# 96 bytes of padding in place of 32 ahead of the constants in a two-layer diffusion backbone

## Chip, cores and metric

One Trainium2 chip, one of its cores. The metric is the device time of one execution in microseconds (us); the median of three runs of the kernel before is 2884.68 us.

## What is computed

The reference is a backbone of two layers over 1024 latent tokens (T) and 256 context tokens (CT), 1280 together (TA), with D = 1024 channels, in float32:

```python
for i in range(DEPTH):                       # 2 layers
    h  = modulate(rmsnorm(x, norm_mix_w[i]), sh_m, sc_m)
    hc = modulate(rmsnorm(ctx, norm_mix_w[i]), shc_m, scc_m)
    y, y_c = ab_mixer(...) if i % 2 == 0 else cd_mixer(...)
    x = x + g_m * y
    ...
    x = x + g_f * swiglu(modulate(rmsnorm(x, norm_ffn_w[i]), sh_f, sc_f), w_gate, w_up, w_down)
    ...                                      # layer 0 does the same for ctx
return rmsnorm(x, final_norm_w)
```

Layer 0 mixes with a gated token MLP and neighbourhood attention (`ab_mixer`), layer 1 with a Fourier transform and gated linear attention (`cd_mixer`). The FFN's hidden width is 2816, 22 slabs of 128.

## The kernel before, in words

**Three matmuls for one.** Every float32 operand of a large product is held as two tiles of type float32r, a high and a low part. `mm3` (lines 45 to 51) issues three matmuls into one PSUM target: `wh` on `xh` (L49), `wh` on `xl` (L50), `wl` on `xh` (L51). In `nc.tensor.matmul(out, wh, xh)` the second argument is the stationary operand, which is loaded into the array ahead of the matmul (LDWEIGHTS), and the third is the moving operand, which streams through it. For most products the weights are stationary, 128 columns of them, and the activations move, 512 columns (a block of 512 tokens) or 256 (the context block). The value products `gv`, `gu`, `av` and `va` have it the other way: slices of the activations are stationary, 256 or 272 columns of weights move.

**Stages** of the program, by the time at which they run: layer 0's norms, projections and gated MLP to about 300 us; attention (`natten`) to 690 us, with the other projections (`qk`) and half of the output product (`ho`) put between its steps by a generator (`s.bg`, `tick`); `out_proj` to 760 us; the first FFN to 1640 us; layer 1's linear attention, `gla_*`, and the Fourier part `fnet` to 2110 us, again with a generator beside them; `out_proj`; the second FFN from 2190 us to the end, with the final norm behind its last blocks. In an FFN (`ffn`, line 330 on) `up` makes the gate and up products (`pg` is the PSUM name of both in the trace) and `down` the product `dn`, whose result is added to `xT` by DVE (`residual`, L316).

**What sets the order.** Each engine executes its instructions in the order of the program; a tile framework adds the waits. The order is that of the Python code with its generators, and none of it depends on addresses.

**Where tiles lie.** Pools are stacks. Those on the left side grow up from the lowest free byte of a partition, those on the right side grow down from byte 229,344. `cp` is the first pool on the left; its first tile is `pad`, 8 floats (32 bytes) that nothing reads (`setup`, line 113), then `ident`, `ones` and the small constants. Behind `cp` on the left come `hm` (the activations `hh`/`hl`, eight pairs of 4 KB; in layer 1 the same places hold `xT`, the Fourier twiddles `tw` and the mixed activations `mixd`) and `hc` (the eight pairs of context activations, 1 KB each, behind a 192-byte tile `cs`). On the right are the weights (`whi`, `wlo`), eight slots of 5 KB (`xT` in layer 0, `mixc` in layer 1, and others) and the FFN's hidden tiles (`hhi`, `hlo`).

The *residue* of an operand is the byte at which it begins in its partition, modulo 128. From the built program:

| operand | first byte before | residue before | residue after |
|---|---|---|---|
| `hh`, `hl`, `mixd` (and `xT`, `tw` in layer 1), left | from 19,872 | 32 | 96 |
| `hc`, left | from 85,600 | 96 | 32 |
| `whi`, `wlo`, right | from 162,272 | 96 | 96 |
| `mixc`, right | from 188,384 | 96 | 96 |
| `hhi`, `hlo` of the FFNs, right | from 85,728 | 96 | 96 |
| `vhi`, `vlo` of the gated MLP (moving in `gt`), right | 120,224 | 32 | 32 |
| `swh`, `swl` (stationary in `gt`), right | 113,792 | 0 | 0 |

The matmuls with float32r operands, by columns and by the residues of the moving and the stationary operand:

| columns | moving, stationary before | after | count | which |
|---|---|---|---|---|
| 512 | 32, 96 | 96, 96 | 4704 | `pg` on `hh`/`hl` 2112, `pg` on `mixd` 1056, `qk` 384, `ho` 384, `op` 192, `gqk` 192, `gf` 192, gates 192 |
| 512 | 96, 96 | the same | 3320 | `dn` 2112, `pg` on `mixc` 1056, `op` 144, `dec` 8 |
| 512 | 32, 0 | the same | 24 | `gt` |
| 256 | 96, 96 | 32, 96 | 1488 | context blocks on `hc`, 1056 of them `pg` |
| 256 | 96, 32 | 96, 96 | 1152 | `gv`, `gu`, `av` and a few `qk`, stationary `hh`/`hl` |
| 256 | 96, 96 | 96, 32 | 288 | the same, stationary `hc` |
| 256 | 32, 96 | 96, 96 | 192 | `y` on `tw` |
| 256 | 96, 96 | the same | 1676 | attention's `sp` and `o`, `dn` of the context, others |

Of the kernel before, what the change touches and what calls it, by code (L numbers as in the profile page):

```python
# [11 lines left out]
F32 = mybir.dt.float32  # L12
# [8 lines left out]
P = 128  # L21
# [48 lines left out]
def psum(s, tag, name=None):  # L70

    if tag != "s":
        return s.ps.tile([P, 512], F32, name=name or tag, tag=tag, bufs=2 if tag == "t" else 1)
    if s.half is None:
        pair = psum2(s, name)
        s.half = pair[:, 512:]
        return pair[:, :512]
    half, s.half = s.half, None
    return half
# [30 lines left out]

def setup(s, a):
    nc, cp = s.nc, s.cp
    cp.tile([P, 8], F32, name="pad")
    s.ident = cp.tile([P, P], F32, name="ident")
    make_identity(nc, s.ident)
    s.ones = cp.tile([P, P], F32, name="ones")
    nc.gpsimd.memset(s.ones, 1.0)
    s.half_neg = cp.tile([P, 16], F32, name="half_neg")
    nc.gpsimd.memset(s.half_neg, -0.5)


    flat = lambda ap, n: bass.AP(tensor=ap.tensor, offset=ap.offset, ap=[[P, n], [1, P]])
    r0 = s.xp.tile([16, P], F32, name="r0")
    nc.sync.dma_start(r0[0:8, :], flat(a["c"], 8))
    nc.sync.dma_start(r0[8:16, :], flat(a["c_ctx"], 8))
    s.cs = s.hc.tile([P, KT, 6], F32, name="cs")
    nc.gpsimd.memset(s.cs, 0.0)
    pt = psum(s, "t", "setup")
    nc.tensor.transpose(pt[:, :16], r0, s.ident[:16, :16])
    nc.scalar.activation(s.cs[:, :, 2:4], pt[:, :16].rearrange("p (s k) -> p k s", s=2), AF.Silu)  # L130

    r1 = s.xp.tile([P, P], F32, name="r1")
    nc.gpsimd.memset(r1, 0.0)
    rows = [("nmw", a["norm_mix_w"], 16), ("nfw", a["norm_ffn_w"], 16), ("dbf", a["cd_decay_b_fwd"], 2),
            ("dbb", a["cd_decay_b_bwd"], 2), ("hnw", a["cd_head_norm_w"], 1), ("sgb", a["ab_sgu_b"], 4)]
    at = 0
    for name, ap, n in rows:
        nc.sync.dma_start(r1[at:at + n, :], flat(ap, n))
        at += n
    r2 = s.xp.tile([96, P], F32, name="r2")  # L140
    nc.sync.dma_start(r2, flat(a["ada_b"], 96))
    pt = psum(s, "t", "setup")
    nc.tensor.transpose(pt[:, :P], r1, s.ident)
    nc.tensor.transpose(pt[:, P:P + 96], r2, s.ident[:96, :96])
    s.cols = cp.tile([P, 41], F32, name="cols")
    nc.vector.tensor_copy(s.cols, pt[:, :41])
    s.adab = cp.tile([P, 96], F32, name="adab")
    nc.vector.tensor_copy(s.adab, pt[:, P:P + 96])
    at = 0
    s.col = {}  # L150
    for name, ap, n in rows:
        s.col[name] = s.cols[:, at:at + n]
        at += n
    s.mod = [cp.tile([P, 48, 2], F32, name=f"mod{l}") for l in range(2)]
    s.acol = [[cp.tile([P, KT, 2], F32, name=f"acol{l}{j}") for j in range(2)] for l in range(2)]
# [1217 lines left out]
def body(ctx, tc, a, out, dbg=None):  # L1373
# [22 lines left out]
    with P_("hc", side="left") as s.hc:  # L1396
# [6 lines left out]
        with ExitStack() as es:  # L1403
# [4 lines left out]
            with R("ld") as ld, R("np0") as s.np_:  # L1408
                s.xp = s.adap = ld
                setup(s, a)  # L1410
                jobs = [q(0), k(0)]
                s.bg = ada(s, a, 0, [1, 0], "pe")
                xin, r = [], {}
                for i in range(TA // P):
                    xin.append(load_x(s, a, i))
                    tick(s)
                    if i == 7:
                        acol(s, 0, 0)
                    if i in (3, 7, 9):
                        blk = BLK[(i - 2) // 3]  # L1420
                        turn_x(s, xin, xT, blk)
                        r[blk] = rstd(s, xT, blk)
                tick(s, 3)
                ws = proj_w(s, a, jobs)
                drain(s)
                hT = [tuple(Cols(m, s.hc.tile([P, CT], F32R, name=f"hc{x}{k}")) for x, m in enumerate(pair))
                      for k, pair in enumerate(alloc_h(s))]
                proj_t(s, a, hT, jobs, pre=lambda blk: norm(s, xT, hT, 0, 0, blk, r[blk]), ws=ws)
                spill(s, xT, xd[0])
# [180 lines left out]
```

## Time and profile before

| | |
|---|---|
| median of 3 runs | 2884.68 us (2879.55 to 2887.2) |
| the profiled execution's own time | 2882.54 us |
| its span, first to last instruction | 2880.6 us |
| granted TensorE clock, mean | 0.991 of full speed |
| PE (matmul) busy | 2779.9 us, 97%, 14927 matmuls |
| DVE / ACT / POOL busy | 54% / 31% / 7% |
| chain that ended last | PE 80%, DVE 8%, ACT 4%, DMA 4%, issue 2% |

How to read it: the span is the profiled execution's time without what lies around it. Matmuls are pipelined and the ends of their records are modelled, so records overlap and a busy PE is not PE at its peak; the distance between the starts of neighbouring matmuls is what a matmul takes of the engine's time. PEld is the loading of stationary operands, which runs beside the matmuls. The chain is followed back from the last instruction, at each step to what released it. The trace names tiles without buffer numbers: `pg<-hh,whi` is a matmul with the stationary operand `whi` and the moving operand `hh` into PSUM tile `pg`.

### The profile page before, as it was taken

How to read it: one execution, taken by the hardware profiler on the slowest of the kernel's cores; microseconds unless marked ns; L12 is line 12 of the kernel's file. 1: busy time of each engine (PE TensorE's matmuls, PEld its weight loads, DVE VectorE, ACT ScalarE, POOL GpSimd, SP SyncE). 2: the span in 40 equal slices, each digit the busy share in tenths (PEclk: the TensorE clock that was granted, in tenths of full speed). 3: DMA queues.
4: the chain of work that ended last, by engine and by line, in shares of the span. 5: the costliest groups of instructions: out<-in, count | busy, mean ns of one | idle time of the engine just before them, and what ended most of it. 6: DMA issues, size and time to landing. Idle time of an engine off the chain costs nothing.

```text
span 2880.6 us, 38369 instructions
## 1 busy us (share of the span) xinstructions
PE 2779.9 (97%) x14927; PEld 2336.3 (81%) x14927; DVE 1550.4 (54%) x2791; ACT 893.1 (31%) x1899; POOL 198.2 (7%) x233
## 2 busy tenths in 40 slices
PE   8999999899999999999999999998999999999998
PEld 3888888787888888888888787787878888888887
DVE  4655777676664643645633466756773333333435
ACT  3442566554311111111111145554251111111112
POOL 0000222221100000000000021212010000000000
PEclk9999999999999999999999999999999999999999
DMA  8545656674231321312211143533621111111111
GB/s 300 169 130 160 180 158 178 205 211 126 81 95 52 96 80 45 103 44 88 88 37 40 35 166 87 161 121 100 222 83 52 44 46 54 48 44 51 52 44 66
DMA packets 285686, 298.50 MB, mean 104 GB/s; under 512 B 33416, under 2 KB 228673, under 8 KB 285505
## 3 DMA queue, kind: packets, MB, share of 16 engines
q1 hardware_dynamic: 285505, 296.06, 34.0%
q8 instruction: 118, 1.93, 0.3%
q14 instruction: 63, 0.52, 0.1%
HBM read 228.09 MB, written 64.49 MB: 102 GB/s over the span
## 4 chain that ended last, share of the span: by engine, by line
PE 80%; DVE 8%; ACT 4%; DMA 4%; issue 2%; POOL 1%; SPq 0%; DVEq 0%; POOLq 0%; ACTq 0%
PE pg L51 13%; PE pg L50 13%; PE pg L49 13%; PE dn L49 6%; PE dn L50 5%; PE dn L51 5%; PE o L750 2%; PE pt L720 1%; DMA adaw<-in_ada_w_dram 1%; PE sp L661 1%; PE qk L49 1%; PE ho L49 1%; PE qk L50 1%; DVE xT L316 1%; DVE wlo L57 1%
## 5 line engine op out<-in xcount | busy, mean ns | idle before, releaser
L56 ACT CAST whi<-wraw 128x1024 fp32r<-128x1024 f32 (+2 forms) x186 | 188.4, 1013 | 687.1 <-PE dn L50 404.2
L316 DVE SCALAR_TENSOR_TENSOR xT<-dn,mod,xT 128x512 f32<-128x512 f32 (+1 forms) x448 | 300.0, 686 | 122.9 <-PE dn L51 121.8
L57 DVE TENSOR_TENSOR wlo<-wraw,whi 128x1024 fp32r<-128x1024 f32 (+2 forms) x186 | 220.3, 1187 | 248.1 <-ACT whi L56 246.6
L49 PE MATMUL dn<-hhi,whi 128*128 128x512 f32 (+1 forms) x896 | 328.3, 367 | 4.6 <-DVE xT L316 3.1
L50 PE MATMUL dn<-hlo,whi 128*128 128x512 f32 (+1 forms) x896 | 327.0, 365 | 0.0
L51 PE MATMUL dn<-hhi,wlo 128*128 128x512 f32 (+1 forms) x896 | 326.7, 365 | 0.0
L346 DVE TENSOR_TENSOR sg<-sg,pg 128x512 f32<-128x512 f32 (+1 forms) x110 | 69.4, 631 | 378.7 <-ACT sg L345 378.6
L51 PE MATMUL pg<-hh,wlo 128*128 128x512 f32 x688 | 272.8, 397 | 0.2
L49 PE MATMUL pg<-hh,whi 128*128 128x512 f32 x688 | 272.5, 396 | 0.0
L50 PE MATMUL pg<-hl,whi 128*128 128x512 f32 x688 | 271.9, 395 | 0.0
L183 DVE SCALAR_TENSOR_TENSOR adaacc<-adaw,cs,adaacc 128x1024 f32<-128x1024 f32 x140 | 175.0, 1280 | 114.5 <-DMA adaw<-in_ada_w_dram 111.1
L345 ACT ACTIVATE sg<-pg 128x512 f32<-128x512 f32 (+1 forms) x110 | 60.8, 552 | 563.1 <-PE pg L51 563.1
L49 PEld LDWEIGHTS dn<-hhi,whi 128*128 128x128 f32 x896 | 168.9, 188 | 36.1 <-DVE xT L316 7.2
L51 PEld LDWEIGHTS dn<-hhi,wlo 128*128 128x128 f32 x896 | 168.9, 188 | 27.3
L50 PEld LDWEIGHTS dn<-hlo,whi 128*128 128x128 f32 x896 | 169.0, 189 | 26.8
L51 PEld LDWEIGHTS pg<-hh,wlo 128*128 128x128 f32 x688 | 129.2, 188 | 32.2 <-DVE wlo L57 1.1
L50 PEld LDWEIGHTS pg<-hl,whi 128*128 128x128 f32 x688 | 129.1, 188 | 30.3
L49 PEld LDWEIGHTS pg<-hh,whi 128*128 128x128 f32 x688 | 129.1, 188 | 30.1
L50 PE MATMUL pg<-mixd,whi 128*128 128x512 f32 x344 | 136.0, 395 | 0.0
L49 PE MATMUL pg<-mixd,whi 128*128 128x512 f32 x344 | 135.5, 394 | 0.0
L51 PE MATMUL pg<-mixd,wlo 128*128 128x512 f32 x344 | 135.5, 394 | 0.0
L49 PE MATMUL pg<-mixc,whi 128*128 128x512 f32 x344 | 134.2, 390 | 0.9 <-DVE xT L316 0.9
(569 smaller groups left out, 6192.0 us busy)
## 6 DMA issues: line engine op xcount, KB each, us to landing
adaw<-in_ada_w_dram SPq DMA_DIRECT2D x96, 512.0 KB, 3.9
wraw<-in_ffn_w_gate_dram SPq DMA_DIRECT2D x44, 512.0 KB, 3.8
wraw<-in_ffn_w_up_dram SPq DMA_DIRECT2D x44, 512.0 KB, 3.8
wraw<-in_ffn_w_down_dram SPq DMA_DIRECT2D x44, 512.0 KB, 3.8
wraw<-in_ab_w_in_dram SPq DMA_DIRECT2D x20, 512.0 KB, 5.5
xd<-xT SPq DMA_DIRECT2D x16, 640.0 KB, 5.8
xs<-xd SPq DMA_DIRECT2D x32, 256.0 KB, 3.3
xd<-xs SPq DMA_DIRECT2D x32, 256.0 KB, 2.8
```

Of the source, the lines that this page charges most:

```text
L49: nc.tensor.matmul(out, wh, xh, start=start, stop=False)
L50: nc.tensor.matmul(out, wh, xl, start=False, stop=False)
L51: nc.tensor.matmul(out, wl, xh, start=False, stop=stop)
L56: s.nc.scalar.copy(hi, src)
L57: (s.nc.gpsimd if eng == "pool" else s.nc.vector).tensor_tensor(lo, src, f32(hi), ALU.subtract)
L183: nc.vector.scalar_tensor_tensor(acc[:, v], w, c, acc[:, v], ALU.mult, ALU.add)
L316: s.nc.vector.scalar_tensor_tensor(xT[k][:, o:o + n], ps, s.mod[l][:, 8 * vec + k, sel:sel + 1], xT[k][:, o:o + n], ALU.mult, ALU.add)
L345: nc.scalar.activation(sg[:, :n], pg[:, :n], AF.Silu)
L346: nc.vector.tensor_tensor(sg[:, :n], sg[:, :n], pu[:, :n], ALU.mult)
L661: nc.tensor.matmul(sp[:, o:o + n], qq[:, x, :], kk[:, t0:t0 + n], start=x == 0, stop=x == 1)
L720: nc.tensor.transpose(pt[:n, jj * P:(jj + 1) * P], y[:, c:c + n], s.ident)
L750: nc.tensor.matmul(o_ps[:, ba * P:bz * P], vv[:n, kt, :], at(x, sl)[:n, 0, ba:bz, :].rearrange("p b q -> p (b q)"), start=q == 0 and x == ...
```

## The change

The unread tile ahead of the constants has 24 floats in place of 8, 96 bytes in place of 32:

```diff
 def setup(s, a):
     nc, cp = s.nc, s.cp
-    cp.tile([P, 8], F32, name="pad")
+    cp.tile([P, 24], F32, name="pad")
     s.ident = cp.tile([P, P], F32, name="ident")
```

Every other tile of the left side begins 64 bytes later; no tile of the right side moves. The instructions and their order are the same on every engine.

## Rows read from the trace of the kernel before

**Rows 1.** The page's head and its section 1, busy us, share and instructions.

```profile
span 2880.6 us, 38369 instructions
PE 2779.9 (97%) x14927; PEld 2336.3 (81%) x14927; DVE 1550.4 (54%) x2791; ACT 893.1 (31%) x1899; POOL 198.2 (7%) x233
```

**Rows 2.** Stretches: us, busy PE, PEld, DVE, ACT, POOL, clock, DMA share, GB/s.

```profile
760.00:1640.00 880.00, 877.16 (x4587) 745.29 (x4586) 432.93 (x566) 144.95 (x203) 0.00 (x0) 1.00 0.23 70
2190.00:2860.00 670.00, 669.96 (x2956) 548.71 (x2955) 252.99 (x323) 113.04 (x152) 1.11 (x2) 1.00 0.15 46
300.00:690.00 390.00, 368.49 (x2387) 323.38 (x2386) 278.83 (x850) 224.15 (x663) 81.80 (x105) 0.99 0.64 186
...
1740.00:2110.00 370.00, 347.16 (x1915) 292.28 (x1914) 252.20 (x519) 181.99 (x433) 55.26 (x63) 0.97 0.47 143
```

**Rows 3.** The chain of waits by line, in 2190 to 2860 us and 300 to 690 us.

```profile
by line: PE pg L50 21.6%; PE pg L49 21.5%; PE pg L51 21.5%; PE dn L50 11.6%; PE dn L49 11.6%; PE dn L51 11.6%; PE ft L1309 0.5%; ACT fsq L1311 0.1%; DVE xT L316 0.1%; DVE fss L1312 0.0%; issue 0.0%; ACTq L1311 0.0%
by line: PE o L750 12.7%; PE pt L720 9.4%; PE sp L661 7.5%; PE qk L49 5.5%; PE qk L50 4.9%; PE qk L51 4.8%; issue 4.0%; DMA wraw<-in_ab_w_out_dram 3.7%; PE ho L49 3.3%; PE ho L50 3.1%; PE ho L51 3.1%; DVE pa L731 2.3%; PE op L50 2.2%; PE op
```

**Rows 4.** Timeline of PE, second FFN: start us, us, engine, line, out<-in (`mixc`, then `mixd`).

```profile
2289.77 0.39 PE L49 MATMUL pg<-mixc,whi 128*128 128x512 f32 x1
...
2295.21 0.39 PE L49 MATMUL pg<-mixd,whi 128*128 128x512 f32 x1
...
2298.48 0.39 PE L51 MATMUL pg<-mixd,wlo 128*128 128x512 f32 x1
```

**Rows 5.** PE's groups by line and shape: count, busy us, mean ns, idle before.

```profile
L51 PE MATMUL pg<-hh,wlo 128*128 128x512 f32 x688 | 272.8, 397 | 0.2
L49 PE MATMUL pg<-hh,whi 128*128 128x512 f32 x688 | 272.5, 396 | 0.0
L49 PE MATMUL dn<-hhi,whi 128*128 128x512 f32 x688 | 268.3, 391 | 3.6 <-DVE xT L316 2.2 <-DVE sg L346 1.4
...
L51 PE MATMUL dn<-hhi,wlo 128*128 128x512 f32 x688 | 267.7, 389 | 0.0
L50 PE MATMUL pg<-mixd,whi 128*128 128x512 f32 x344 | 136.0, 395 | 0.0
...
L50 PE MATMUL pg<-mixc,whi 128*128 128x512 f32 x344 | 134.5, 391 | 0.0
```

**Rows 6.** Timeline of PE: five `gt` matmuls, the first and the next behind them.

```profile
182.67 0.39 PE L49 MATMUL gt<-vhi,swh 128*128 128x512 f32 x1
...
183.83 0.30 PE L49 MATMUL av<-whi,hh 128*128 128x256 f32 x1
```

**Rows 7.** Timeline of PE, first FFN: `pg` on `hh`/`hl`, then `pg` on `hc`.

```profile
1058.83 0.39 PE L50 MATMUL pg<-hl,whi 128*128 128x512 f32 x1
...
1061.39 0.28 PE L49 MATMUL pg<-hc,whi 128*128 128x256 f32 x1
...
1062.93 0.28 PE L50 MATMUL pg<-hc,whi 128*128 128x256 f32 x1
```

**Rows 8.** Timeline of PE, 256 columns: `gv` with stationary `hh`, `y` with moving `tw`.

```profile
115.48 0.28 PE L49 MATMUL gv<-whi,hh 128*128 128x256 f32 x1
...
117.84 0.28 PE L51 MATMUL gv<-whi,hl 128*128 128x256 f32 x1
...
2045.58 0.28 PE L51 MATMUL y<-tw,zl 128*128 128x256 f32 x1
...
2046.75 0.40 PE L49 MATMUL ho<-mixd,whi 128*128 128x512 f32 x1
```

**Rows 9.** DVE's L316 in the two FFN stretches: min/median/max ns, forms, idle before.

```profile
L316 DVE SCALAR_TENSOR_TENSOR xT<-dn,mod,xT x241: 473/743/752, 814.3 to 1638.2; 128x512 f32<-128x512 f32 x81, 128x256 f32<-128x256 f32 x40
...
  PE dn L51: 48.1, 102
...
L316 DVE SCALAR_TENSOR_TENSOR xT<-dn,mod,xT x174: 475/751/753, 2204.7 to 2859.5; 128x512 f32<-128x512 f32 x168, 128x256 f32<-128x256 f32 x6
...
  PE dn L51: 67.7, 117
```

## What I predict

> **What bounds the kernel now.** I read the head of the page first, for the share of each engine, then a table of stretches, then the chain of waits inside two stretches, and last the timeline of TensorE, because the change moves bytes and no instruction and can only show in how far apart equal instructions start.
>
> The page says that TensorE is busy 97% of a span of 2880.6 us [rows 1]. [...] In the attention stretch (300 to 690 us) it is 368.5 of 390, in the linear-attention and Fourier stretch (1740 to 2110 us) 347.2 of 370, with some 22 us without a matmul in each. The chain agrees: in the second FFN nearly all of it is matmuls `pg` and `dn` (three times 21.5% and three times 11.6%), while in the attention stretch the longest entries are small matmuls and issue and DMA each hold some 4% [rows 3]. So in the FFNs the time is the number of matmuls times the distance between their starts; elsewhere a part of what PE saves will be waited away.
>
> PE's busy figures are no help for the price: each record is longer (0.39 us) than the distance to the next start, since matmuls overlap. The distance is what counts. In one chain of the second FFN, 24 matmuls on `mixc` start from 2289.77 to 2295.21 us, 5.44 us or 0.2267 us each; then, with the weights in the same tiles and PSUM targets of the same kind, 14 matmuls on `mixd` take until 2298.48 us, 3.27 us or 0.2336 us each [rows 4]. Their rows are alike in engine, line and shape; what differs is where the moving operand lies: `mixc` begins at residue 96 of 128, as the weights do, `mixd` at residue 32 (the table of residues above). The first FFN shows the same: 11 matmuls on `hh` and `hl` (residue 32) from 1058.83 to 1061.39 us are 0.2327 us apart [rows 7]. Over all records the mean durations repeat it [rows 5]: `pg` on `hh` 396 and 397 ns and on `mixd` 395 ns, but `dn` 389 and 391 ns and `pg` on `mixc` 391 ns, whose operands both begin at 96.
>
> **Is it the residue, or the place?** `mixc` and the FFN's hidden tiles lie high in SBUF, `hh` and `mixd` low, so a difference by region would look the same. One small group speaks to that: the `gt` matmuls of the gating read a moving tile at residue 32 that lies at 120,224 bytes, above `dn`'s tiles of the second FFN, with weights at residue 0. Five starts from 182.67 to 183.83 us are 0.232 us apart [rows 6], the slow distance. That favours the residue, but on five instructions, with a distance of 32 bytes and not of 64, so I leave a chance for the region.
>
> **The change part by part.**
>
> *512-column matmuls, FFN.* Of the 4704 that go from 32 against 96 to 96 against 96, 3168 are `pg`: 2112 on `hh` and `hl`, 1056 on `mixd`. The gain of one lies between 4 ns (the smallest difference of mean durations, 395 against 391 [rows 5]) and 7 ns (0.2336 against 0.2267 us [rows 4]); in the first FFN it is 0.2327 against 0.2267, 6 ns [rows 4, 7]. I take 6 ns, the middle of the three and the one from the stage with the most of them. 3168 x 6 ns = 19.0 us, all on the path, since nothing else ends the chain there. Bounds 12.7 us (4 ns) and 22.2 us (7 ns).
>
> *512-column matmuls elsewhere.* 4704 - 3168 = 1536: projections `qk`, `gqk`, `gf`, gates, and the output products `ho` and `op`. At 6 ns they free 9.2 us of PE. The attention and later stretches have PE without a matmul for 22 of 390 and 23 of 370 us [rows 2], so most of the time there the next matmul is ready; but the small matmuls between them wait for softmax and for DMAs, and a projection that ends sooner then only lengthens such a wait. I count 60%, 5.5 us; bounds 0 and 1536 x 7 ns = 10.8 us.
>
> *256-column matmuls.* The context tiles `hc` go the other way, from 96 to 32: 1488 matmuls of 256 columns. And 1152 matmuls of 256 columns get their stationary operand (slices of `hh` and `hl`) at 96 in place of 32. The trace has all three pairs at 256 columns: 96 on 96 (`pg` on `hc`) 13 starts in 1.54 us, 0.1185 us [rows 7]; moving 96 on stationary 32 (`gv`) 20 starts in 2.36 us, 0.1180 us; moving 32 on stationary 96 (`y`) 10 starts in 1.17 us, 0.1170 us [rows 8]. They lie within 1.5 ns, and with the other sign: the unequal pairs are not slower here. The first edit is then worth 1488 x -1.5 = -2.2 us, the second 1152 x +0.5 = +0.6 us. Differences this small are about the 0.01 us to which starts are shown, so I take 0 for both together. Bounds: -3 us, and +10 us if the 7 ns of a 512-column matmul were paid by each of the 1488.
>
> *Other engines.* Tiles of the left side that DVE, ScalarE and GpSimd touch move by 64 bytes too. DVE's residual update writes `xT` at residue 96 in the first FFN and at 32 in the second; its 512-column form is the slowest in both, 752 and 753 ns [rows 9], so I cost these moves at nothing. Were they dearer, DVE's idle time in the FFNs would cover it: before that line alone it waits 48.1 and 67.7 us for PE [rows 9]. No DMA, wait or instruction is added, moved or removed, no tile changes its size, and the 64 bytes come out of free space.
>
> *Sum.* 19.0 + 5.5 + 0 = 24.5 us. The profiled execution took 2882.54 us, 1.9 us more than its span; 2882.5 - 24.5 = 2858.0 us. That execution lies 2.1 us under the median of the runs shown (2884.68), so the forecast for the median is **2860 us**, 0.85% less.
>
> **The rivals.**
>
> *Waited away outside the FFNs.* All that is gained outside is lost to later waits, and `hc` costs some ns. For it: the chain of the attention stretch with its DMA and issue pieces [rows 3]. Against: PE has a matmul running 94% of that stretch [rows 2]. 3168 matmuls at 5 to 6 ns less 1488 at up to 4 ns is 10 to 19 us: 2866 to 2875 us.
>
> *Nothing happens.* If the 6 ns belong to the region of SBUF, or to something that `mixd` and `hh` share other than the residue, the tiles stay where they are but for 64 bytes and the time is 2884.7 us, with -3 to +3 us from the 256-column forms. For it: all but the `gt` rows allow it. Against: the `gt` rows [rows 6], and that within a chain the distance changes at the very matmul at which the tile does [rows 4]. [...]
>
> *Equal residues are the costly case.* At 256 columns the equal pair has the longest distance, 0.1185 against 0.1170 us [rows 7, 8]. If that is the effect of the residue at any width, and the 6 ns of the 512-column forms are one of region (as in the rival above), then the 4704 matmuls that the change makes equal lose, for twice the columns, 2 x 1.5 = 3 ns each: 4704 x 3 ns = +14.1 us, less 2.2 us for `hc`: 2884.7 + 11.9 = 2897 us. It decides if a 512-column `pg` on `mixd` comes out over 0.2336 us. Against it: `mixc` and `dn` are equal pairs now and are the fast ones [rows 4, 5], and `gt`.
>
> **How the numbers follow.** A difference under 0.3%, 8.7 us, is about what a measurement of this kernel can't tell from none, so faster means under 2876 us and slower over 2893 us. Chances: the forecast 0.72, waited away 0.14, nothing 0.10, costly 0.04. The first two are faster: **0.86**; nothing is the same: **0.10**; the last is slower: **0.04**. The range: its low end takes all bounds to the good, 22.2 + 10.8 + 3 = 36 us, 2849 us, less 2 us for the spread of single runs: 2847. Its high end takes in the second case: 2874 us. That leaves out the last two cases and a small part of the others, not more than 2 in 10.
>
> **What would show it.** Right: `pg` on `hh` and `mixd` with mean durations of 389 to 391 ns like `mixc` and `dn`; starts 0.2267 us apart through the change from `mixc` to `mixd`; the two FFN stretches shorter by some 12 and 6 us (2112 and 1056 matmuls at 6 ns), with the number of instructions and PE's order as before; `hc` within 2 ns of 0.1185 us. The 60% is wrong if PE's idle time outside the FFNs stays as it is (all 9 us are kept) or grows by 9 us (none is). The prediction fails if `pg` on `mixd` keeps its 395 ns, or if `hc`'s distance rises towards 0.125 us.

## The result, and the profile after

Six executions of each kernel, side by side: **2862.51 us** after (2850.39 to 2863.98) against 2881.53 us before (2875.99 to 2887.2). The ratio is 0.9926, with a 95% interval of 0.9906 to 0.9946: 0.74% faster, 16 to 27 us. The forecast was 2860 us in a range of 2847 to 2874.

The head, section 1 and the shares of the chain on the page of the kernel after, to be held against [rows 1]:

```profile
span 2862.0 us, 38369 instructions
PE 2758.1 (96%) x14927; PEld 2339.4 (82%) x14927; DVE 1551.5 (54%) x2791; ACT 892.2 (31%) x1899; POOL 196.5 (7%) x233
...
PE 79%; DVE 9%; DMA 5%; ACT 4%; issue 3%; POOL 1%; SPq 0%; DVEq 0%; ACTq 0%; POOLq 0%
```

The number of instructions is the same, weight loading (PEld) is as busy as before, and PE's matmuls alone are shorter, by 21.8 us of busy time. PE's groups by line and shape in the kernel after (count, busy us, mean ns, idle before), as in [rows 5]:

```profile
L51 PE MATMUL pg<-hh,wlo 128*128 128x512 f32 x688 | 269.2, 391 | 0.6 <-DVE wlo L57 0.6
L49 PE MATMUL pg<-hh,whi 128*128 128x512 f32 x688 | 269.0, 391 | 0.0
...
L51 PE MATMUL dn<-hhi,wlo 128*128 128x512 f32 x688 | 267.6, 389 | 0.0
L50 PE MATMUL pg<-mixd,whi 128*128 128x512 f32 x344 | 134.3, 390 | 0.0
...
L50 PE MATMUL pg<-mixc,whi 128*128 128x512 f32 x344 | 133.8, 389 | 0.0
```

`pg` on `hh` went from 396 and 397 ns to 391, on `mixd` from 395 to 390; `dn`, which the change does not touch, stayed. The same passage from `mixc` to `mixd` in the timeline of the second FFN, after, as in [rows 4]:

```profile
2277.47 0.39 PE L49 MATMUL pg<-mixc,whi 128*128 128x512 f32 x1
...
2282.91 0.39 PE L49 MATMUL pg<-mixd,whi 128*128 128x512 f32 x1
...
2288.35 0.39 PE L49 MATMUL pg<-mixc,whi 128*128 128x512 f32 x1
```

24 matmuls on `mixc` take 5.44 us and 24 on `mixd` take 5.44 us: 0.2267 us each on both sides of the seam at which the distance was 0.2267 and then 0.2336 us.

Two tables of stretches, first before and then after, cut at the first start of `sp`, the last of `o`, the first of `pg`, `va`, `dec`, `z`, `pg` on `mixc`, and the last `ft`; columns as in [rows 2]. First the kernel before, its attention, first FFN, linear attention and second FFN:

```profile
303.10:659.60 356.50, 337.58 (x2254) 299.25 (x2253) 260.00 (x823) 214.87 (x649) 79.81 (x101) 0.99 0.65 187
...
720.60:1673.70 953.10, 943.56 (x4884) 796.83 (x4883) 481.64 (x645) 181.50 (x265) 20.99 (x19) 1.00 0.23 69
...
1747.60:2001.30 253.70, 232.72 (x1269) 194.65 (x1269) 171.72 (x358) 143.45 (x369) 53.59 (x62) 0.96 0.37 110
...
2131.80:2873.70 741.90, 738.20 (x3290) 604.55 (x3290) 288.12 (x383) 139.38 (x199) 10.64 (x13) 1.00 0.15 47
```

The kernel after, with `out_proj` between attention and first FFN:

```profile
304.00:660.90 356.90, 337.52 (x2253) 299.83 (x2253) 260.36 (x823) 214.50 (x649) 78.66 (x101) 0.99 0.65 186
660.90:724.00 63.10, 59.33 (x298) 49.69 (x297) 41.92 (x62) 26.15 (x39) 8.14 (x6) 0.95 0.35 109
724.00:1667.40 943.40, 931.70 (x4885) 797.21 (x4883) 481.31 (x645) 181.30 (x265) 20.93 (x19) 1.00 0.23 70
...
1741.20:1991.10 249.90, 228.34 (x1269) 193.74 (x1269) 172.69 (x358) 143.16 (x368) 53.21 (x62) 0.97 0.38 111
...
2121.40:2855.20 733.80, 730.06 (x3289) 605.58 (x3290) 288.15 (x384) 139.24 (x199) 10.59 (x13) 1.00 0.16 48
```

The first FFN is 9.7 us shorter, the second 8.1. Attention, which has its share of the 512-column matmuls, is not shorter at all. `out_proj` is 63.1 us in place of 61.0: its granted clock is 0.95 where it was 1.00, with 6.8 us at half the full clock. At that level 512-column matmuls of this trace start 0.426 us apart (`qk`, 8 distances from 297.41 to 300.82 us), so the 6.8 us cost about half of that, an estimate from 0.426 and 0.227 us. Such pieces come and go between executions: the mean granted clock of the six after lies between 0.988 and 0.992. Linear attention is 3.8 us shorter, of which 2 to 3 us are clock (0.97 for 0.96 of some 250 us).

A distance, in what follows, is the time from the start of one matmul to the start of the next, averaged over all neighbours between which nothing waited, at full clock (over 245 ns for 512 columns and 128 ns for 256 counts as a wait). In the two profiles:

| matmul | before, ns | after, ns |
|---|---|---|
| 512 columns: `pg` on `hh`/`hl` | 233.3 | 226.9 |
| `pg` on `mixd` | 233.3 | 226.7 |
| `pg` on `mixc` (residues unchanged) | 227.7 | 226.7 |
| `qk`; `ho`; `op` on `hh`/`hl` | 233.1; 233.0; 233.3 | 229.9; 230.4; 227.0 |
| 256 columns: `pg` on `hc` | 118.6 | 117.6 |
| `gv`, `gu`, `av` (stationary `hh`/`hl`) | 117.2 | 119.5 |
| `y` | 116.5 | 119.1 |

### The profile page after: what moved, and what is told of

It reads as the page before. It is cut to its first block, busy times and chain, and to the rows that moved or that the text cites. A ratio compares the mean times of both kernels' runs of the same rounds, so it can differ in the third digit from the quotient of the medians.

```text
span 2862.0 us, 38369 instructions
## 1 busy us (share of the span) xinstructions
PE 2758.1 (96%) x14927; PEld 2339.4 (82%) x14927; DVE 1551.5 (54%) x2791; ACT 892.2 (31%) x1899; POOL 196.5 (7%) x233
## 4 chain that ended last, share of the span: by engine, by line
PE 79%; DVE 9%; DMA 5%; ACT 4%; issue 3%; POOL 1%; SPq 0%; DVEq 0%; ACTq 0%; POOLq 0%
PE pg L51 12%; PE pg L50 12%; PE pg L49 12%; PE dn L49 5%; PE dn L50 5%; PE dn L51 5%; PE o L750 2%; PE pt L720 1%; DMA adaw<-in_ada_w_dram 1%; DVE xT L316 1%; DVE adaacc L183 1%; DVE wlo L57 1%; PE ho L49 1%; PE sp L661 1%; PE qk L49 1%
## 5 line engine op out<-in xcount | busy, mean ns | idle before, releaser
L316 DVE SCALAR_TENSOR_TENSOR xT<-dn,mod,xT 128x512 f32<-128x512 f32 (+1 forms) x448 | 299.7, 686 | 122.4 <-PE dn L51 120.3
L49 PE MATMUL dn<-hhi,whi 128*128 128x512 f32 (+1 forms) x896 | 328.6, 368 | 6.3 <-DVE xT L316 4.7
L50 PE MATMUL dn<-hlo,whi 128*128 128x512 f32 (+1 forms) x896 | 326.9, 365 | 0.0
L49 PE MATMUL pg<-hh,whi 128*128 128x512 f32 x688 | 269.0, 391 | 0.0
L50 PE MATMUL pg<-hl,whi 128*128 128x512 f32 x688 | 268.3, 390 | 0.0
L49 PEld LDWEIGHTS dn<-hhi,whi 128*128 128x128 f32 x896 | 168.9, 189 | 39.6 <-DVE xT L316 11.1
L50 PEld LDWEIGHTS dn<-hlo,whi 128*128 128x128 f32 x896 | 169.0, 189 | 26.3
L50 PEld LDWEIGHTS pg<-hl,whi 128*128 128x128 f32 x688 | 129.5, 188 | 26.0
L49 PEld LDWEIGHTS pg<-hh,whi 128*128 128x128 f32 x688 | 129.5, 188 | 25.9
L49 PE MATMUL pg<-mixc,whi 128*128 128x512 f32 x344 | 133.9, 389 | 0.9 <-DVE xT L316 0.9
L50 PE MATMUL pg<-mixd,whi 128*128 128x512 f32 x344 | 134.3, 390 | 0.0
L50 PE MATMUL pg<-mixc,whi 128*128 128x512 f32 x344 | 133.8, 389 | 0.0
```

The source lines that it names most:

```text
L49: nc.tensor.matmul(out, wh, xh, start=start, stop=False)
L50: nc.tensor.matmul(out, wh, xl, start=False, stop=False)
L316: s.nc.vector.scalar_tensor_tensor(xT[k][:, o:o + n], ps, s.mod[l][:, 8 * vec + k, sel:sel + 1], xT[k][:, o:o + n], ALU.mult, ALU.add)
```

## The experiments

Three theories were tested. A: a 512-column matmul is slow when moving and stationary operand begin 64 bytes apart in 128. B: the residue of the moving operand alone decides, 96 good and 32 bad. C: something else that comes with moving the left side.

**The same equality at the other residue, and the mirror of the change.** The first kernel leaves the left side at 32 and moves the right side from 96 to 32; the second moves both sides, so that they are unequal again with `hh` at 96 and the weights at 32.

```diff
 # e1_both32: pad as before; e2_mirror: pad [P, 24] as in the change
+    pool("rp", side="right").tile([P, 16], F32, name="rpad")   # ahead of the right side's pools
```

> Padding back to 32 bytes (left side at residue 32), and 64 unread bytes ahead of the first pool of the right side, so that weights, mixc and the hidden tiles lie at 32 too: all 8024 pairs of 512 columns are 32 on 32. Theory A (the pair: a 512-column matmul is slow where moving and stationary operand begin 64 bytes apart modulo 128): all of them 0.227 us apart, mean durations 389 to 391 ns, time that of the changed kernel, 2862 us within 5. Theory B (the moving operand alone: residue 96 is good, 32 is bad): all of them 0.233 us apart, dn and pg on mixc up from 390 to 395 ns, 3320 x 6.6 ns = 22 us over the kernel before, 2903 us. Theory C (the 64 bytes act through something else of the left side, as DVE's or DMA's accesses): as the kernel before, 2881 us.

> Padding 96 bytes (left side at residue 96) and 64 unread bytes ahead of the right side (weights, mixc, hidden tiles at 32): the pairs of the kernel before with both sides turned round. Theory A: pg on hh and mixd slow again at 0.233 us and 395 ns, dn and pg on mixc fast (0.227 us, 390 ns), time 2881 us within 6. Theory B: pg on hh and mixd fast (390 ns), dn and pg on mixc slow (395 ns); in the FFNs 3168 faster and 3168 slower ones, so the time alone, 2880 us or so, would not tell; the durations do. Theory C: as the changed kernel, 2862 us.

e1_both32: 2858.27 us against 2881.07, ratio 0.9916 (0.9901 to 0.9931), as fast as the change. e2_mirror: 2876.89 us, ratio 0.998 (0.997 to 0.999), nearly all of the gain lost. PE's groups by shape of e1_both32:

```profile
L49 PE MATMUL pg<-hh,whi 128*128 128x512 f32 x688 | 268.9, 391 | 0.0
...
L50 PE MATMUL pg<-mixd,whi 128*128 128x512 f32 x344 | 134.3, 391 | 0.0
```

and of e2_mirror:

```profile
L49 PE MATMUL pg<-hh,whi 128*128 128x512 f32 x688 | 272.8, 397 | 0.0
...
L51 PE MATMUL dn<-hhi,wlo 128*128 128x512 f32 x688 | 267.8, 389 | 0.0
L49 PE MATMUL pg<-mixd,whi 128*128 128x512 f32 x344 | 135.8, 395 | 0.0
L49 PE MATMUL pg<-mixc,whi 128*128 128x512 f32 x344 | 135.4, 394 | 0.9 <-DVE xT L316 0.9
...
L50 PE MATMUL pg<-mixd,whi 128*128 128x512 f32 x344 | 134.6, 391 | 0.0
```

`hh` at 32 is fast beside weights at 32 and `hh` at 96 slow beside weights at 32: B falls, and of A it holds that equal pairs are fast. Two rows of the mirror A does not explain. `mixc` is an equal pair there (32 on 32) and has 394 ns at L49: it follows `mixd` in each chain, and part of the slow spacing goes on behind the seam (230.8 ns on average for the first ten matmuls on `mixc`, 226.7 from the eleventh on); the spacing of a matmul depends also on what ran ahead of it. And `mixd`, 64 bytes apart as in the kernel before, has 391 ns at L50 where [rows 5] had 395; the next run says more of this.

**The left side moved by 128 bytes.** All residues modulo 128 are as before, all left tiles elsewhere.

```diff
-    cp.tile([P, 8], F32, name="pad")
+    cp.tile([P, 40], F32, name="pad")
```

> Padding 160 bytes: the left side moves by 128 bytes and stays at residue 32. Theories A and B: as the kernel before, 2881 us within 5, pg on mixd 395 ns. Theory C (moving the left side does it, or its exact place): something else than 2881, 2862 us if any move does it.

2881.02 us, ratio 1.0001 (0.9989 to 1.0014). Moving the left side by itself gains nothing that the time shows, so C falls. PE's groups by shape of e3_pad160:

```profile
L49 PE MATMUL pg<-hh,whi 128*128 128x512 f32 x688 | 272.8, 397 | 0.0
...
L49 PE MATMUL pg<-mixd,whi 128*128 128x512 f32 x344 | 135.8, 395 | 0.0
L49 PE MATMUL pg<-mixc,whi 128*128 128x512 f32 x344 | 135.4, 394 | 0.9 <-DVE xT L316 0.9
...
L50 PE MATMUL pg<-mixd,whi 128*128 128x512 f32 x344 | 134.6, 391 | 0.0
```

But these are the rows of the mirror, and not those of the kernel before, which A had expected. In the timeline the fifth and the twenty-fourth matmul of a chain on `mixd` in e3_pad160:

```profile
2250.43 0.39 PE L50 MATMUL pg<-mixd,whi 128*128 128x512 f32 x1
...
2254.78 0.39 PE L51 MATMUL pg<-mixd,wlo 128*128 128x512 f32 x1
```

19 distances in 4.35 us are 0.2289 us each, where the kernel before had 0.2333. What e3_pad160 shares with the mirror shows when the first bytes are counted modulo 256: `hh` and `mixd` begin 64 bytes *below* the weights in the kernel before (160 and 224), at the same byte after the change and in e1_both32, and 64 bytes *above* them in the mirror (224 and 160) and in e3_pad160 (32 and 224). So the settled distance of 512 columns is 233.3 ns for 64 below, 226.7 for equal and 228.9 for 64 above. The residue modulo 128, by which A is put, cannot tell the first from the last. No run was made to test this reading; the table that follows bears it out in one execution. It also means that e3_pad160 did not leave all distances alone: by them it should be a few us faster than the kernel before, as the mirror is. Its ten runs had a mean granted clock of 0.988 and those of the kernel before 0.990, some 12 us more at the half level, which may hide that; this is an estimate from the clocks, not a shown cause.

**A table of residues.** A kernel that leaves out the whole computation and has chains of 48 matmuls, with operands at chosen offsets of two tiles of random float32r values:

```python
nc.tensor.matmul(pt[:, :n], w[:, k + P*(j % 7):k + P*(j % 7 + 1)], m[:, o + 512*(j % 4):o + 512*(j % 4) + n], ...)
```

> Leaves out the whole computation: two tiles of random numbers, groups of 48 to 60 float32r matmuls in a row with 128 columns of weights each, the start of the moving operand at residues 0 to 112 in steps of 16 and that of the stationary at 96, 32 or 0; 512 and 256 columns; two groups in which the stationary operand's residue alternates between 96 and 32, one PSUM target for each. Theory A: 32 on 96, 96 on 32 and 64 on 0 slow (0.233 us), equal pairs 0.227 us; what the steps between give is open; at 256 columns equal pairs 0.1185 us, unequal ones 0.117 us. Theory B: 32 slow and 96 fast whatever the stationary one is. In the alternating groups, if the weights loaded during a matmul (those of the next) collide with its stream, the matmul ahead of a load at the other residue is the slow one; if its own weights count, the other.

Mean distance in ns from the fifth matmul of a chain on, 128 stationary columns:

| columns, stationary at | moving at 0 | 16 | 32 | 48 | 64 | 80 | 96 | 112 |
|---|---|---|---|---|---|---|---|---|
| 512, 96 | 234.2 | 233.4 | 233.4 | 234.6 | 233.4 | 226.7 | 227.2 | 231.6 |
| 512, 32 | 233.2 | | 226.8 | | 233.3 | | 228.9 | |
| 512, 0 | 227.1 | | 233.3 | | 228.9 | | 233.5 | |
| 256, 96 | 118.7 | 119.2 | 113.4 | 119.3 | 118.4 | 117.1 | 120.0 | 118.7 |
| 256, 32 | | | 120.0 | | | | 117.8 | |

The tile views of four chains of this kernel (min/median/max ns, first and last start):

```profile
L69 PE MATMUL w_mg_sg<-m,w x48: 387/389/398, 91.1 to 101.8; 128*128 128x512 f32 x48
...
L69 PE MATMUL w_mc_sg<-m,w x48: 388/393/399, 46.6 to 57.6; 128*128 128x512 f32 x48
...
L69 PE MATMUL h_mg_sg<-m,w x48: 280/283/284, 235.7 to 241.4; 128*128 128x256 f32 x48
...
L69 PE MATMUL h_mc_sg<-m,w x48: 276/276/285, 213.2 to 218.6; 128*128 128x256 f32 x48
```

`mg`, `mc` are a moving operand at 96 and 32, `sg` a stationary one at 96, `w` 512 and `h` 256 columns. Between first and last start lie 47 distances: 10.7 against 11.0 us for 512 columns, and 5.7 against 5.4 us for 256. So equal is fast at 512 columns whatever the residue (0, 32 and 96 were tried), and at 256 columns it is the other way round: equal is the slowest, 32 on 96 the fastest (96 on 32 gave 117.8 ns here and 113.3 in the next kernel). Two entries do not fit "64 apart is slow": 96 on 32 and 64 on 0 have 228.9 ns. In both the moving operand begins 64 bytes above the stationary one, as in the mirror and e3_pad160, which have the same 228.9 ns; in 32 on 96 it begins 64 below. Chains that alternate between weights at 32 and 96 gave 228.4 to 231.5 ns for either, so whether the running or the next weights count was not settled.

**Weight loads of fewer columns, finer residues, short chains.** The same kind of kernel, computation left out again.

```diff
-            nc.tensor.matmul(pts[q][:, :n], w[:, k + P * (j % 7):k + P * (j % 7 + 1)],
+            nc.tensor.matmul(pts[q][:cols, :n], w[:, k + P * (j % 7):k + P * (j % 7) + cols],
...
+        for i in range(8):
+            group(f"short_m{L[x]}", 8 * x, 96, 512, 6)
+            group(f"between_m{L[x]}", 96, 96, 256, 3)
```

> Leaves out the whole computation, as the table before it: groups of float32r matmuls on random numbers. (1) Stationary operand of 128, 64, 32 and 4 columns, moving operand of 512 columns at residue 96 or 32, stationary at 96. [...] (2) Residues of the moving operand in steps of 8 around that of the stationary: the fast ones lie in a band that begins some 16 bytes below it, as 80 on 96 was 226.7 ns and 112 on 96 231.6 ns. (3) Runs of only 6 matmuls of 512 columns between three of 256: if the missing gain outside the FFNs is one of settling, the equal pair is about 230 ns in such short runs against 233 ns for 32 on 96, not 227; if it is waits alone, 227 against 233. 80 on 96 is open.

PE's groups by shape in e5_widths (`mm` moving at 96, `me` at 32, `sm` stationary at 96; full, half and few are 128, 64 and 4 stationary columns; short is chains of six):

```profile
L69 PE MATMUL short_me<-m,w 128*128 128x512 f32 x48 | 12.5, 395 | 0.0
L69 PE MATMUL short_mm<-m,w 128*128 128x512 f32 x48 | 12.5, 395 | 0.0
...
L69 PE MATMUL full_me_sm<-m,w 128*128 128x512 f32 x48 | 11.4, 394 | 0.0
...
L69 PE MATMUL few_me_sm<-m,w 128*4 128x512 f32 x48 | 11.3, 394 | 0.0
...
L69 PE MATMUL few_mm_sm<-m,w 128*4 128x512 f32 x48 | 11.3, 394 | 0.0
L69 PE MATMUL half_mm_sm<-m,w 128*64 128x512 f32 x48 | 11.2, 392 | 0.0
...
L69 PE MATMUL full_mm_sm<-m,w 128*128 128x512 f32 x48 | 11.1, 389 | 0.0
```

| stationary columns | equal (96 on 96), ns | 64 apart (32 on 96), ns |
|---|---|---|
| 128 | 226.8 | 233.3 |
| 64 | 230.1 | 232.7 |
| 32 | 231.7 | 231.7 |
| 4 | 231.7 | 231.7 |
| 128, chains of six between 256-column matmuls | 232.5 | 234.2 |

With 32 and with 4 stationary columns the residue has no effect (231.7 ns for both pairs); with 64 it makes 2.6 ns, with 128 6.5 ns. That it acts through the weight load is my reading of this and not shown by itself. Nor does the distance fall with the number of stationary columns: with 4 it is 231.7 ns, and 128 at the equal residue make it *shorter* by 5 ns, at the other 1.6 ns longer. The smooth band of good residues below 96 that I had expected did not show either: in steps of 8 from 64 to 120 on 96 only 96 itself was fast (227.3 ns, the others 231.6 to 236.6). 80 on 96 gave 236.6 ns here and 226.7 in the table above, so the two residues alone do not set the distance. The last line is what matters for this kernel: in chains of six the equal pair gains 1.7 ns and not 6.5.

**80 bytes of padding.** Meant to try 80 on 96 in the kernel itself.

```diff
-    cp.tile([P, 8], F32, name="pad")
+    cp.tile([P, 20], F32, name="pad")
```

> Padding of 80 bytes: hh, hl, mixd at residue 80, hc at 16, the right side at 96 as before. In the table 80 on 96 came out at 226.7 ns from its first matmuls on, where 96 on 96 needs about eight to settle. Theory A with settling: pg 389 ns in the FFNs, and the short runs outside (qk, ho) nearer to 227 than 230 ns, so 2 to 4 us less than the changed kernel, 2859 us, if the 256-column forms (16 on 96, 96 on 80) stay within 1 ns of now. Theory A as equality alone: 80 is not 96, so slow, 233 ns and 2881 us.

In the built program the tile of 80 bytes takes 96, so this is the changed kernel once more: 2865.07 us, ratio 0.9942 (0.9922 to 0.9962). 80 on 96 was not tried in the kernel.

**The other sign at 256 columns, used.** The last three runs, on one chip: the changed kernel again, then with the weights of the value products 64 bytes later in their slots (`gv`, `gu`, `av` 64 apart again), then also the context columns of the first FFN's hidden tiles.

```diff
 # e8_values64, against the changed kernel
-    lo = wslab(s, w[0:D // 2, c0:c0 + n], KT // 2, n)
+    lo = wslab(s, w[0:D // 2, c0:c0 + n], KT // 2, n, None, 16)
 # e9_all64, besides
-    places = hidden(s)
+    places = hidden(s, (P, TA + 32)) if l == 0 else hidden(s)
```

> The changed kernel once more, beside the two that follow: 2862 us, ratio to the kernel before 0.992 to 0.994 by every theory.

> The changed kernel, and in the value products (gv, gu, av: 256 moving columns of weights on stationary hh and hl) the weights begin 64 bytes later in their slots: 1152 pairs go from 96 on 96 to 32 on 96, and 288 from 96 on 32 to 32 on 32. Theory A with the sign that the table has for 256 columns (64 apart 113.3 ns where it has settled, equal 120): the 1152 come down from 119.4 to between 117.5 and 113.5 ns, the 288 go up by 2 to 5 ns; 1 to 5 us less than the changed kernel where PE is the limit, less where the projections wait. Equality is good at any width (rival): 2 to 5 us more.

> As the one before, and in the first FFN the context columns of the hidden tiles begin 64 bytes later, so that the 528 matmuls dn of 256 columns go from 96 on 96 to 32 on 96. Theory A with that sign: dn of 256 columns from 119.6 to between 117.7 and 113.3 ns, 1 to 3 us less than the kernel before it in this list; together 2 to 8 us less than the changed kernel. Rival: slower by as much.

| run | median, us | ratio to before |
|---|---|---|
| e7_after_again | 2865.45 | 0.9933 (0.9918 to 0.9949) |
| e8_values64 | 2863.47 | 0.993 (0.9915 to 0.9946) |
| e9_all64 | 2866.38 | 0.9937 (0.992 to 0.9954) |

The distances moved as meant: in e8_values64 `gv`, `gu` and `av` on `hh` and `hl` from 119.5 to between 117.2 and 117.8 ns, the 288 on `hc` up by some 3 ns to 119; in e9_all64 the context's `dn` from 119.6 to 117.3. The time did not, by anything that these intervals resolve. In e9_all64 the 512-column `dn` became slower, though its own residues stayed, in its groups by shape

```profile
L49 PE MATMUL dn<-hhi,whi 128*128 128x512 f32 x688 | 269.3, 393 | 5.6 <-DVE xT L323 4.1 <-DVE sg L354 1.4
```

where it had 392 ns after the change. By the distances its 1056 matmuls in the first FFN went from 227.4 to 230.6 ns, 3.4 us lost for 1.2 us gained on the context's. No version measurably faster than the changed kernel was found.

## Why the prediction was right, step by step

**The mechanism was right in what the forecast needs.** Equal residues make the long matmuls shorter (e1, e2, and 226.8 to 227.2 ns in the table of residues, where 64 apart has 228.9 to 233.4), and the signs named beforehand came: 390 and 391 ns on `mixd` and `hh`, 0.2267 us through the seam, `hc` within 2 ns of 0.1185 us, PE's order unchanged, the two FFNs shorter by 9.7 and 8.1 us for "some 12 and 6". "Nothing happens" fell with e1_both32, in which the left side stays in its place, the right side moves, and the gain is the same: it is where the two begin relative to each other, and not the region. Too coarse was the residue modulo 128: 64 bytes below and 64 above are alike modulo 128, but have two distances, 233.3 and 228.9 ns (e3_pad160, the mirror, the table). That the change made the pairs equal modulo 256 too was not looked at beforehand; should a pair 128 bytes apart be slow, which no run shows, the forecast had luck in this. "Equal residues are the costly case" fell at 512 columns, though its observation at 256 is true.

Where the two operands begin matters at 512 columns by 6.5 ns with 128 stationary columns, by 2.6 ns with 64, and not at all with 32 or 4 (e5_widths). What in the engine makes it so, no run shows.

**Where the gain lies.** Lengths of the stages in two profiles of the old residues (e3's the same modulo 128 alone) and four with equal ones, us:

| | before | e3 | after | e6 | e7 | e1 | difference of means |
|---|---|---|---|---|---|---|---|
| first FFN | 953.1 | 952.3 | 943.4 | 943.2 | 944.1 | 941.2 | -9.7 |
| second FFN | 741.9 | 740.6 | 733.8 | 733.6 | 733.9 | 733.6 | -7.5 |
| all else | 1178.7 | 1178.0 | 1178.0 | 1178.7 | 1179.2 | 1174.4 | -0.8 |

**The FFN term, 19.0 us, measured 17.2.** In the second FFN the forecast was 1056 x 6 = 6 us; it gave 7.5, because a matmul gained 6.6 ns, 7.0 us in all, and because the 1056 on `mixc` gained up to a nanosecond too: the slow spacing no longer runs on behind the seam. In the first FFN it was 2112 x 6 = 13 us. The distances did give that: 2112 x 6.4 ns = 13.5 us, and 1.1 us from `hc`. The stage gave 9.7. "All on the path, since nothing else ends the chain there" was too simple: PE's idle time in this stage is 9.5 us before and 11.5 in e3_pad160, and 11.7 after, 12.3, 15.2 and 11.6 in e6, e7 and e1, some 2 us more on average. The wait that is named, in PE's waits of the kernel after:

```profile
PE dn L49 <- DVE xT L316: 4.7, 11, 1.0
```

was 3.1 us, 8 times before (but 4.5 us, 11 times in e3): a `dn` waits for DVE's residual update to be done with its PSUM target, and comes to it sooner now. Old and new overlap here, so this is the likely place for some 2 us, not a shown one; the rest of the difference is that e3's `pg` on `hh`, 64 above the weights and not 64 below, stood at 231.7 ns where before had 233.3, and the clock: TensorE was granted the half level for 3.4 and 0 us of this stage in the two old profiles and for 6.8, 6.8, 0 and 3.4 us in the new ones, on average some 1.3 us of time that the new ones lost.

**The step that failed: "I count 60%, 5.5 us" for the 1536 matmuls outside the FFNs.** All that lies outside the FFNs became 0.8 us shorter, within the spread of a few us between executions of one layout. And the reason given for the 40% that was taken off, waits, is not the main one: outside the FFNs PE was without a matmul for 81 and 79 us in the two old profiles, and 82, 85, 82 and 77 in the new ones. By the sign set beforehand an unchanged idle time meant that all 9 us are kept; that sign misled, since PE's busy time hardly fell either. Two things were missed:

- The 6 ns hold for long chains only. Two chains of twelve `qk` matmuls in the timelines of PE in the attention stretch; first before, the fourth and the last:

```profile
399.63 0.39 PE L49 MATMUL qk<-hh,whi 128*128 128x512 f32 x1
...
401.50 0.39 PE L51 MATMUL qk<-hh,wlo 128*128 128x512 f32 x1
```

  then after, the second and the last:

```profile
400.91 0.40 PE L50 MATMUL qk<-hl,whi 128*128 128x512 f32 x1
...
403.22 0.39 PE L51 MATMUL qk<-hh,wlo 128*128 128x512 f32 x1
```

  8 distances in 1.87 us, 0.2338 us each, became 10 in 2.31 us, 0.231 each. By the place in its chain, the mean distance of a 512-column matmul after the change is 232.0 ns for the first, 230.9 for the fourth, 228.3 for the seventh, 226.7 from the thirteenth on. A matmul far inside the `pg` chains, from whose rows the 6 ns came, has settled; outside the FFNs half of the chains are six long or shorter. e5_widths has the same by itself, 1.7 ns in chains of six. By the distances the 1536 freed some 6 us and not 9.2.
- "256-column matmuls: 0". The 1488 on `hc` gained 1.0 ns in the FFN and some 3 ns outside it, 2.4 us in all, near the forecast's -2.2, and the 288 with stationary `hc`, which the forecast left out, some 3 ns, 0.9 us. But the 1152 with stationary `hh` and `hl` lost 2.2 ns each, 2.5 us, and `y` 2.6 ns, 0.5 us, all of it outside the FFNs. [Rows 7, 8] had shown the sign; the +0.6 us in the text used 0.5 ns, the difference of 0.1185 and 0.1180 us from some 20 starts, where the settled difference is four times that. The pair of [rows 7] was a poor model for it: `hc` lies at the weights' residue modulo 128, but 128 bytes from it modulo 256 (118.6 ns); in e3_pad160, where it is equal modulo 256, it has 119.9 ns.

So outside the FFNs 6 us from the 1536 and 2 us from `hc`, less 3 us lost, leave some 5 us by the distances of before and after; those of e3_pad160 and after leave about nothing, so that the mean of the two old profiles leads one to expect some 2. PE's busy time there fell by 2 us on average (1098 to 1096 us), the idle time rose by 1.3, and neither is resolved against the spread.

**The sum** by stages is -18.0 us, by the medians -19.0, by the ratio -21.3; 24.5 were forecast. It came within the range because each mis-sized term was small. The high end's own case, "waited away outside the FFNs", gives the better account of the size (10 to 19 us), though not of the cause.

**What stays open.** Why an equal residue with 128 stationary columns makes a 512-column matmul faster (226.7 against 233.3 ns), and a 256-column one slower (120.0 against 113.4 in the table); why 64 bytes above and 64 below differ, and what a pair 128 bytes apart gives at 512 columns, which was not tried; whether the running or the next weights count; why the same pair can sit at two distances for a whole chain (80 on 96 at 512 columns: 226.7 and 236.6 ns; 96 on 32 at 256: 117.8 and 113.3).

## What to carry to other kernels

When equal instructions have two spacings in one stage, compare where their operands begin, with the sign and modulo 256: in long chains of 512-column float32r matmuls with 128 stationary columns, moving and stationary operands at the same byte modulo 256 were worth 2.8% of each matmul here against 64 bytes below (226.7 and 233.3 ns), and 1% against 64 above (228.9 ns), for the price of a pad. Read distances between starts, from chains as long as those to be costed, and price the short chains by themselves (1.7 ns in chains of six, where long ones have 6.5). At 256 columns the sign was the other way here (`gv`, `gu`, `av` from 117.2 to 119.5 ns); this pad served one shape and took from the other, so count both.

## What the runs showed of the hardware that was not expected

- The time from one matmul to the next depends on the pair of start addresses: with 128 stationary columns, in long chains, for 512 columns 226.7 ns where both begin at the same byte modulo 256, 228.9 where the moving operand begins 64 bytes above the stationary one and 233.3 where it begins 64 below; for 256 columns 120.0 ns for equal and 113.4 for 64 below (e4_table), the other way round.
- A 512-column matmul can be faster with 128 stationary columns than with 4: 226.8 ns at the equal residue, 231.7 with 4 (e5_widths).
- An equal pair takes a dozen matmuls to come to its short distance (232.0 ns for the first, 226.7 from the thirteenth), and a chain can carry its spacing over into the next tile's matmuls: `mixc` in the mirror, 394 ns at L49 with equal residues.
